# Values' projection moved to the head of a decoder layer, and its first weights loaded by a second queue

## The chip, the cores and the metric

The kernel runs on one core of one Trainium2 chip. The metric is device time in microseconds (us) of one execution. In the trace PE is TensorE, ACT is ScalarE, DVE is VectorE, POOL is GpSimd and SP is SyncE, which only starts transfers (DMAs) here.

## What is computed

One decoder layer for 256 rows of 1024 numbers, all in float32. Cut to what matters for the change:

```
def rmsnorm(x, g):
    y = x * rsqrt(mean(x * x, axis=-1, keepdims=True) + 1e-6)
    return y * g
...
hn = rmsnorm(x, norm_mix[i])
(aq, ak, av, bq, bkc, bvc, bks, bvs, bkw, bvw, bg, cq, ck, cv, mg) = split(hn @ w_in[i])
o_a = dilated_mixer(heads(aq), heads(ak), heads(av), tbl_a)
o_b = nsa_mixer(...)
o_c = moba_mixer(...)
merged = gates[0] * (o_a @ wb[:r0]) + gates[1] * (o_b @ wb[r0:r1]) + gates[2] * (o_c @ wb[r1:])
x = x + merged @ w_out[i]
x = x + conv_ffn(rmsnorm(x, norm_ffn[i]), ...)
return rmsnorm(x, norm_final)
```

The head of the kernel makes `aq` and `ak` (mixer A's queries and keys, 768 columns), `bkc` and `bvc` (256 columns), and `av` with `bvs` (512 columns: the values). Then A's attention begins.

## The kernel before

**Splitting.** Products run in fp32r. Each float32 operand is split into a high part (a copy rounded to fp32r, by ACT) and a low part (what the rounding left, by DVE), and a product is high by high, low by high and high by low: three matmuls. This holds for x and for the weights.

**Units.** Weights arrive as units of up to 1 MB (`Unit`, L205): one transfer into a `raw` tile (4 of them), the high part on ACT (`hi`, L220), the low part on DVE (`lo`, L224), into two pairs of `whi`/`wlo` tiles. So unit n+2 can be split only when PE has finished with unit n, and its transfer needs a free `raw` tile. SP issues all the transfers in program order.

**The head (L242 to L419).** It is written out by hand: inside `tc.manual_schedule` the instructions of PE, ACT, DVE and POOL stand on each engine in the order of the text. SP loads x's two halves of 128 rows (x0, x1), a small table for the position bias, then `a0` as two halves of 512 KB, `a1` as two halves, and `a2`. PE does 9 idle matmuls (`keep_warm`), then turns x by 16 transposes (`turn`, L282) into four PSUM tiles that each hold two chunks of 128 columns for all 256 rows. `hi_part` and `lo_part` (L312, L318) multiply by the norm's weights and split; the norm's 1/rms is not yet in. `a0_products` (L322) makes the first two of A's six chunks (128 columns each, with the weights as the stationary operand and 256 rows moving) in an order that follows the weights' arrival. POOL makes three of `a0`'s low parts. A chunk's result is multiplied by the row's 1/rms afterwards (`by_rows_rstd`, L290). The four chunks of `a1` and `a2` come from `chunk3_T` (L294): 24 matmuls of 256 columns each. Beside them x is normed into `h_parts` (`normed_rows`, `normed_hi`, `normed_lo`, L388 to L396), which every later projection reads.

**After the head** a list scheduler sets the order from the program's text and its own costs. Unit `kvc` gives two chunks by `chunk3_T` (L479), then `V1 = proj_V("v1", 512, "V1")` (L488) makes the values by rows: `by_rows` (L441) uses x's normed parts as the stationary operand and 512 weight columns as the moving one, 48 matmuls by `mm3` (L237). Then A's scores (L508), DVE's sum with the bias and maximum (L515), the exponentials on ACT (L586), transposes (L522), and the products with V1 (L541). The projections for mixer B (`chunk_T`, L421, one 512-column matmul for both parts of x and one of 256) lie between them and give PE work while DVE and ACT do A's softmax.

Of the kernel before, what the change touches and what calls it, by code (L numbers as in the profile page):

```python
# [16 lines left out]
P = 128  # L17
WARM = 9
NORMED = 3
S = 256  # L20
# [48 lines left out]
def _unit_list():  # L69

    rows = [(0, D)]
    out = [(f"a{i}", "w_in", rows, [(C_AQ + 256 * i, 256)]) for i in range(3)]
    out.append(("kvc", "w_in", rows, [(C_BKC, 256)]))
    out += [(f"v1{i}", "w_in", [(512 * i, 512)], [(C_AV, 384), (C_BVS, 128)]) for i in range(2)]
# [55 lines left out]
def decoder_layer(ctx: ExitStack, tc, x, small_b, table, w1, wts, norms, out):  # L130
# [12 lines left out]
    for t in range(NT):  # L143
        nc.sync.dma_start(xs[:, t, :], x[t * P:(t + 1) * P, :])
    g_mix, g_ffn = xs[:, 0, D:D + KC], xs[:, 1, D:D + KC]
# [59 lines left out]
    class Unit:  # L205


        def __init__(self, name, cuts=1):
# [42 lines left out]
    def s_tile():  # L251
# [12 lines left out]
    x_hi, x_lo = [raw_parts[:, :, i, :] for i in range(2)]  # L264
    xn = [act_pool.tile([P, D], F32, name=f"xn{t}") for t in range(NT)]
    turned = [p.tile([P, 512], F32, name=n).rearrange("p (c q) -> p c q", c=2)
              for p, n in ((ps_t, "t"), (ps_t, "t"), (ps_o, "o"), (ps_o, "o"))]
    xT = [turned[c // 2][:, c % 2, :] for c in range(KC)]
    tb = mix.tile([P, 4, S], F32, name="gl", bufs=4).rearrange("p a b -> p (a b)")[:32, :R_N]
    nc.sync.dma_start(tb, table)  # L270

    T = qkv.tile([P, 16, 256], F32, name="T")
# [30 lines left out]
    with tc.manual_schedule(engines={mybir.EngineType.Activation, mybir.EngineType.DVE, mybir.EngineType.Pool,  # L303
                                     mybir.EngineType.PE}):
        def split_hi(i, eng):
            sl = slice(i * 512, (i + 1) * 512)
            if eng == "v":
                nc.vector.tensor_copy(u_a0.parts[0][:, sl], u_a0.raw[:, sl])
            else:
                nc.scalar.activation(u_a0.parts[0][:, sl], u_a0.raw[:, sl], AF.Copy)  # L310

        def hi_part(c, eng):  # L312
            if eng == "v":
                nc.vector.tensor_scalar_mul(x_hi[:, c, :], xT[c], g_mix[:, c:c + 1])
# [19 lines left out]
        for c in (0, 1):  # L334
            hi_part(c, "v")
        for c in (2, 3):
            hi_part(c, "a")
        hi_part(4, "v")
        split_hi(0, "v")
        split_hi(1, "a")  # L340
        u_a0.lo(0, 4, nc.gpsimd)
        u_a0.lo(1, 4, nc.gpsimd)
        hi_part(5, "v")
        for c in (6, 7):
            hi_part(c, "a")
        split_hi(2, "v")
        split_hi(3, "a")
        a0_products(0, x_hi, range(6))
        ss = square_mean(xs[:, 1, 0:D], xn[1], "m1")
        for c in range(4):  # L350
            lo_part(c)
        a0_products(0, x_hi, range(6, KC))
        a0_products(1, x_hi, range(2))
        a0_products(0, x_lo, range(3))
        a0_products(1, x_hi, range(2, 4))
        u_a0.lo(2, 4, nc.gpsimd)
        rs.append(rstd_of([ss], "m1"))
        for i in range(2):
            u_a1.hi(i, 2)
        for c in range(4, KC):  # L360
            lo_part(c)
# [8 lines left out]
        u_a0.lo(3, 4)  # L370
        a0_products(0, x_lo, range(3, KC))
# [3 lines left out]
        a0_products(1, x_hi, range(4, KC))  # L375
        for i in range(2):
            u_a1.lo(i, 2)


        whole = [mix.tile([P, 4, S], F32, name="gl", bufs=4) for _ in range(2)]  # L380
        h_parts = act_pool.tile([P, KC, 2, S], F32R, name="hn")
        h_hi, h_lo = h_parts[:, :, 0, :], h_parts[:, :, 1, :]

        def weighted_rows(i):
            for c in range(4 * i, 4 * i + 4):
                nc.scalar.activation(whole[i][:, c % 4, :], xT[c], AF.Copy, scale=g_mix[:, c:c + 1])
# [11 lines left out]
        def projected(u, c):  # L398
            return chunk3_T(lambda part, k: u.views[part][:, k, c * P:(c + 1) * P], x_hi, x_lo)

        weighted_rows(0)
        nc.scalar.activation(rows_m, pt[:, :S], AF.Copy)
        u_a2.hi(0, 2)
        for c in range(2):
            by_rows_rstd(c, a0_ps[c])
        weighted_rows(1)
        u_a2.hi(1, 2)
        normed_rows(0)
        by_rows_rstd(2, projected(u_a1, 0))
        normed_rows(1)  # L410
        normed_hi(0)
        for i in range(2):
            u_a2.lo(i, 2)
# [673 lines left out]
```

## Time and profile before

| | us |
|---|---|
| median of 3 runs | 424.87 (424.62 to 425.62) |
| the profiled execution, its own time | 424.76 |
| its span in the trace | 423.0 |
| PE busy in the span | 412.4 |
| DVE busy | 313.2 |
| ACT busy | 256.2 |
| first product of a projection starts on PE | 9.22 |
| A's first scores start | 44.49 |

All times of rows count from the start of the span. The profiled execution took 1.76 us more than its span. PE's busy time counts pipelined matmuls with modelled ends, so a row's duration is longer than the step from one matmul to the next; a step is read from the starts of neighbouring rows.

### The profile page before, as it was taken

Reading aid. Unit: us, or ns where it says so; the run is one execution under the profiler, and the core shown is the slowest. Engines: PE = TensorE matmul, PEld = TensorE weight load, DVE = VectorE, ACT = ScalarE, POOL = GpSimd, SP = SyncE. Lnnn points to the kernel's source line nnn. Section 1 sums busy time; section 2 is a strip of 40 time slices with the busy share of each in tenths; the row PEclk is TensorE's granted clock in tenths of the full one; section 3 lists DMA queues with packets and bytes.
Section 4 is the critical chain, followed back from the end, with each engine's and each line's share of the span. In section 5 each row is a group of like instructions: output and inputs, shape, how many; then the busy total and the mean of one; then the engine's idle time right before and its main releaser. Section 6 shows DMA issues by size and latency. Waiting matters only on the chain.

```text
span 423.0 us, 6337 instructions
## 1 busy us (share of the span) xinstructions
PE 412.4 (98%) x2407; PEld 347.8 (82%) x2407; DVE 313.2 (74%) x624; ACT 256.2 (61%) x451; POOL 18.3 (4%) x28
## 2 busy tenths in 40 slices
PE   8999999999999999999999999999999999999993
PEld 7998778776667888878788998988888888888883
DVE  3996653788784888434753899998797797887765
ACT  5843283547787855555434889467476576584633
POOL 2500010120000000000000000000000000000001
PEclk9999999999999999999999999999999999999998
DMA  8999419532227793645350465565652743800002
GB/s 279 416 375 407 146 34 354 198 131 100 101 100 248 292 381 109 229 184 198 107 192 0 149 253 198 200 251 200 245 212 105 283 187 110 299 0 2 0 2 99
DMA packets 12750, 78.00 MB, mean 184 GB/s; under 512 B 1408, under 2 KB 1424, under 8 KB 4912
## 3 DMA queue, kind: packets, MB, share of 16 engines
q1 hardware_dynamic: 12144, 75.48, 47.8%
q0 software_dynamic: 576, 2.12, 1.4%
q8 instruction: 19, 0.31, 0.3%
q14 instruction: 11, 0.09, 0.1%
HBM read 76.52 MB, written 1.07 MB: 183 GB/s over the span
## 4 chain that ended last, share of the span: by engine, by line
PE 82%; DVE 8%; ACT 5%; DMA 2%; issue 2%; SPq 0%; POOLq 0%; POOL 0%; ACTq 0%
PE g L988 12%; PE g L239 10%; PE g L240 10%; PE g L238 10%; PE g L990 6%; PE acc L238 6%; PE acc L240 6%; PE acc L239 6%; PE g L298 3%; DVE wlo L226 2%; PE g L888 2%; PE o L541 2%; DMA raw<-in_wts_dram 2%; PE g L426 2%; PE g L300 1%
## 5 line engine op out<-in xcount | busy, mean ns | idle before, releaser
L226 DVE TENSOR_TENSOR wlo<-raw,whi 128x1024 fp32r<-128x1024 f32 (+2 forms) x131 | 154.1, 1201 | 41.0 <-ACT whi L222 40.6
L222 ACT ACTIVATE whi<-raw 128x1024 fp32r<-128x1024 f32 (+2 forms) x130 | 130.2, 1040 | 50.5 <-PE g L240 34.3
L988 PE MATMUL g<-parts,whi 128*128 128x512 f32 x256 | 89.4, 396 | 0.0
L990 PE MATMUL g<-parts,wlo 128*128 128x256 f32 x256 | 66.2, 279 | 0.0
L988 PEld LDWEIGHTS g<-parts,whi 128*128 128x128 f32 x256 | 46.7, 188 | 9.2
L990 PEld LDWEIGHTS g<-parts,wlo 128*128 128x128 f32 x256 | 48.2, 188 | 2.8
L239 PE MATMUL g<-wlo,hn 128*128 128x512 f32 (+1 forms) x128 | 50.0, 391 | 0.0
L240 PE MATMUL g<-whi,hn 128*128 128x512 f32 (+1 forms) x128 | 50.0, 391 | 0.0
L238 PE MATMUL g<-whi,hn 128*128 128x512 f32 (+1 forms) x128 | 49.8, 390 | 0.0
L967 DVE SCALAR_TENSOR_TENSOR cy<-xn,small_b,cy 128x255 f32<-128x255 f32 (+1 forms) x88 | 41.5, 480 | 9.0 <-ACT cy L965 8.0
L238 PE MATMUL acc<-whi,fl 128*128 128x512 f32 (+1 forms) x88 | 34.2, 389 | 0.1
L239 PE MATMUL acc<-wlo,fh 128*128 128x512 f32 (+1 forms) x88 | 34.0, 386 | 0.0
L240 PE MATMUL acc<-whi,fh 128*128 128x512 f32 (+1 forms) x88 | 34.0, 386 | 0.0
L965 ACT ACTIVATE cy<-xn,small_b 128x256 f32<-128x256 f32 x44 | 25.8, 598 | 7.4 <-DVE xn L997 7.4
L239 PEld LDWEIGHTS g<-wlo,hn 128*128 128x128 f32 x128 | 24.1, 188 | 5.1 <-issue 0.9
L240 PEld LDWEIGHTS g<-whi,hn 128*128 128x128 f32 x128 | 24.1, 188 | 4.2 <-issue 0.2
L238 PEld LDWEIGHTS g<-whi,hn 128*128 128x128 f32 x128 | 24.1, 189 | 4.0 <-ACT whi L222 0.2
L426 PE MATMUL g<-hn,whi 128*128 128x512 f32 x72 | 26.2, 405 | 0.0
L996 ACT ACTIVATE xn<-g 128x256 f32<-128x256 f32 x32 | 12.2, 380 | 22.2 <-PE g L988 22.2
L428 PE MATMUL g<-hn,wlo 128*128 128x256 f32 x72 | 19.9, 292 | 0.0
L997 DVE TENSOR_TENSOR xn<-g,xn 128x256 f32<-128x256 f32 x32 | 13.5, 421 | 8.3 <-ACT xn L996 8.3
L240 PEld LDWEIGHTS acc<-whi,fh 128*128 128x128 f32 x88 | 16.5, 188 | 3.4
(213 smaller groups left out, 698.6 us busy)
## 6 DMA issues: line engine op xcount, KB each, us to landing
raw<-in_wts_dram SPq DMA_DIRECT2D x61, 1024.0 KB, 4.8
gl<-in_w_dram SPq DMA_DIRECT2D x8, 512.0 KB, 7.6
raw<-in_wts_dram SPq DMA_DIRECT2D x5, 512.0 KB, 7.4
raw<-in_wts_dram SPq DMA_DIRECT2D x2, 804.0 KB, 9.0
T<-tvd POOLq DMA_DIRECT2D x1, 1280.0 KB, 16.3
xs<-in_x_dram SPq DMA_DIRECT2D x2, 516.0 KB, 3.8
out_dram<-raw SPq DMA_DIRECT2D x4, 256.0 KB, 2.1
T<-tvd POOLq DMA_DIRECT2D x1, 768.0 KB, 9.6
```

What stands on the lines that cost most here:

```text
L222: nc.scalar.activation(self.parts[0][:, sl], self.raw[:, sl], AF.Copy)
L226: return (eng or nc.vector).tensor_sub(self.parts[1][:, sl], self.raw[:, sl], self.parts[0][:, sl].bitcast(F32))
L238: nc.tensor.matmul(ps, al, bh, start=start, stop=False)
L239: nc.tensor.matmul(ps, ah, bl, start=False, stop=False)
L240: nc.tensor.matmul(ps, ah, bh, start=False, stop=stop)
L426: hi = lambda: nc.tensor.matmul(ps, view(0, k), h_parts[:, k].rearrange("p a q -> p (a q)"), start=k == 0, stop=k == KC - 1)
L428: lo = lambda: nc.tensor.matmul(ps[:, :S], view(1, k), h_hi[:, k, :], start=False, stop=False)
L965: on_act.append(nc.scalar.activation(y, u, AF.Identity, bias=vec_c[:, 3, ch:ch + 1], scale=vec_c[:, 2, ch:ch + 1]))
L967: nc.vector.scalar_tensor_tensor(y[:, sh:], u[:, :S - sh], vec_c[:, w, ch:ch + 1], y[:, sh:], op0=ALU.mult, op1=ALU.add)
L988: hi = lambda: nc.tensor.matmul(ps, u[0][:, k, cols], h_parts[:, k].rearrange("p a q -> p (a q)"), start=k == 0, stop=k == KC - 1)
L990: lo = lambda: nc.tensor.matmul(ps[:, :S], u[1][:, k, cols], h_parts[:, k, 0, :], start=False, stop=False)
L997: nc.vector.tensor_add(v, ps[:, :S], part)
```

## The change

The values' projection becomes the first one. Units `v10` and `v11` (each 512 of the 1024 rows of the weights by 512 columns) are laid out and loaded first; the first half of `v10` is issued by ACT's queue, while SP issues x0, x1, the second half of `v10`, the table, `v11`, and later `a0`, `a1`, `a2` whole. Each half of x is now turned by itself: `turned[t]` has two PSUM tiles of four chunks for 128 rows; `weighted(t, i)` (DVE) multiplies four chunks by the norm's weights into SBUF, `raw_hi_part` (ACT) and `raw_lo_part` (DVE) split them. PE multiplies x0's first two chunks with `v10` before it turns x1. The values are scaled by 1/rms on ACT as they leave PSUM. A's six chunks then all come from the normed rows `h_parts`: `chunk_products` uses 8 matmuls of 512 columns and 8 of 256 a chunk in place of 24 of 256, and `chunk_sum` adds the two halves (one instruction on ACT, one on DVE). POOL makes no low parts. `proj_V` for V1 is gone from its old place.

```diff
-WARM = 9
+WARM = 8
+PAUSE = 2
...
-    out = [(f"a{i}", "w_in", rows, [(C_AQ + 256 * i, 256)]) for i in range(3)]
+    out = [(f"v1{i}", "w_in", [(512 * i, 512)], [(C_AV, 384), (C_BVS, 128)]) for i in range(2)]
+    out += [(f"a{i}", "w_in", rows, [(C_AQ + 256 * i, 256)]) for i in range(3)]
...
-                nc.sync.dma_start(self.raw[:, sl], src[:, sl])
+                (nc.sync if i else first).dma_start(self.raw[:, sl], src[:, sl])
...
+    turned = [[p.tile([P, 512], F32, name=n).rearrange("p (c q) -> p c q", c=4) for _ in range(2)]
+              for p, n in ((ps_t, "t"), (ps_o, "o"))]
...
+    load_x(1)
+    u_v = [Unit("v10", cuts=2, first=nc.scalar)]
     nc.sync.dma_start(tb, table)
-    u_a0 = Unit("a0", cuts=2)
-    u_a1 = Unit("a1", cuts=2)
-    u_a2 = Unit("a2")
+    u_v.append(Unit("v11"))
...
+        def weighted(t, i):
+            nc.vector.tensor_mul(whole[i][:, :, t * P:(t + 1) * P], turned[t][i],
+                                 g_mix[:, 4 * i:4 * i + 4, None].to_broadcast([P, 4, P]))
...
+        def value_products(t, ks, part):
+
+            for k in ks:
+                u = u_v[k // 4]
+                for a in (raw_hi, raw_lo)[:2 - part]:
+                    nc.tensor.matmul(V1_ps[t], a[:, k, t * P:(t + 1) * P], u.views[part][:, k % 4, :],
+                                     start=part == 0 and a is raw_hi and k == 0, stop=part == 1 and k == KC - 1)
...
+        def chunk_products(u, c):
+
+            ps = psg.tile([P, 512], F32, name="g")
+            cols = slice(c * P, (c + 1) * P)
+            for k in range(KC):
+                nc.tensor.matmul(ps, u.views[0][:, k, cols], h_parts[:, k].rearrange("p a q -> p (a q)"),
+                                 start=k == 0, stop=False)
+            for k in range(KC):
+                nc.tensor.matmul(ps[:, :S], u.views[1][:, k, cols], h_hi[:, k, :], start=False, stop=k == KC - 1)
+            return ps
...
         keep_warm(WARM)
-        rs = [rstd_of([square_mean(xs[:, 0, 0:D], xn[1], "m0")], "m0")]
         turn(0)
+        weighted(0, 0)
+        raw_hi_part(0, 0)
+
+        nc.vector.tensor_copy(u_v[0].parts[0][:, 0:512], u_v[0].raw[:, 0:512])
+        u_v[0].hi(1, 4)
+        raw_lo_part(0, 0)
+        for i in range(2):
+            u_v[0].lo(i, 4)
+        s0 = square_mean(xs[:, 0, 0:D], xn[1], "m0")
+        keep_warm(PAUSE)
+        value_products(0, range(2), 0)
         turn(1)
         nc.tensor.matmul(pt[:16, :384], tb[:, R_RB:R_RB + 16], tb[:, R_OH:R_OH + 384], start=True, stop=True)
...
+        weighted(1, 0)
+        raw_hi_part(1, 0)
+        weighted(0, 1)
+        raw_lo_part(1, 0)
+        value_products(1, range(2), 0)
...
-
-    V1 = proj_V("v1", 512, "V1")
```

**Place 1: PE at the start of the program.** `g<-tt` are the idle matmuls, `<-ident,xs` the transposes, `gl 16x384` the product with the bias table. Before:

```order
L288 MATMUL g<-tt 128x128 x9
L284 MATMUL t<-ident,xs 128x128 x4
L284 MATMUL o<-ident,xs 128x128 x4
L284 MATMUL t<-ident,xs 128x128 x4
L284 MATMUL o<-ident,xs 128x128 x4
L332 MATMUL g<-gl 16x384
L325 MATMUL g<-parts,whi 128x256
L325 MATMUL s<-parts,whi 128x256
```

and with the change:

```order
L298 MATMUL g<-tt 128x128 x8
L294 MATMUL t<-ident,xs 128x128 x8
L298 MATMUL g<-tt 128x128 x2
L329 MATMUL g<-whi,parts 128x512 x4
L294 MATMUL o<-ident,xs 128x128 x8
L375 MATMUL g<-gl 16x384
L329 MATMUL s<-whi,parts 128x512 x4
L329 MATMUL g<-wlo,parts 128x512 x2
L329 MATMUL s<-wlo,parts 128x512 x2
```

The first four products now stand ahead of x1's transposes and of the table's product, which moved behind them.

**Place 2: DVE while the values are multiplied.** `parts` is x's split, `gl` the weighted rows, `hn` the normed split, `wlo` a weight's low part. Before, from the low parts of x on:

```order
L319 SCALAR_TENSOR_TENSOR parts<-t,xs,parts 128x256 x4
L177 TENSOR_SCALAR msm_221<-ssm_196 128x1
L319 SCALAR_TENSOR_TENSOR parts<-o,xs,parts 128x256 x4
L363 TENSOR_TENSOR tt<-g,gl 16x384
L226 TENSOR_TENSOR wlo<-raw,whi 128x512
L226 TENSOR_TENSOR wlo<-raw,whi 128x1024 x2
L292 SCALAR_TENSOR_TENSOR aT_130<-g,xn_105 128x256
L292 SCALAR_TENSOR_TENSOR aT_131<-s,xn_105 128x256
L389 TENSOR_TENSOR gl<-gl,xn_105 128x1024
```

and with the change, from just behind `weighted(1, 0)`, the first instruction that reads x1's transposes, to the low parts of `a0` (the last row's third is `a1`'s):

```order
L312 TENSOR_TENSOR gl<-t,xs 128x4x128
L321 TENSOR_TENSOR parts<-gl,parts 128x4x128
L312 TENSOR_TENSOR gl<-o,xs 128x4x128
L230 TENSOR_TENSOR wlo<-raw,whi 128x512 x2
L181 TENSOR_SCALAR msm_188<-ssm_154 128x1
L321 TENSOR_TENSOR parts<-gl,parts 128x4x128 x2
L181 TENSOR_SCALAR msm_198<-ssm_192 128x1
L400 TENSOR_TENSOR tt<-g,gl 16x384
L230 TENSOR_TENSOR wlo<-raw,whi 128x1024 x2
L333 TENSOR_TENSOR gl<-gl,xn_105 128x1024 x2
L340 TENSOR_TENSOR hn<-gl,hn 128x4x256 x2
L230 TENSOR_TENSOR wlo<-raw,whi 128x1024 x3
```

The norming of x (`gl<-gl,xn` and `hn<-gl,hn`) stood between results of A's chunks; now it stands ahead of `a0`'s low parts, and so ahead of A's first chunk.

**Place 3: PE where A's scores begin** (`s<-aT`; `hn,whi 128x256` are products of `kvc`). Before, the values' products end there:

```order
L238 MATMUL g<-whi,hn 128x512
L239 MATMUL g<-wlo,hn 128x512
L240 MATMUL g<-whi,hn 128x512
L508 MATMUL s<-aT_133,aT_130 128x128 x2
L508 MATMUL s<-aT_133,aT_130 128x256 x2
L426 MATMUL g<-hn,whi 128x512
L428 MATMUL g<-hn,wlo 128x256 x2
```

and with the change:

```order
L350 MATMUL g<-hn,wlo 128x256 x8
L304 MATMUL g<-hn,whi 128x256 x16
L306 MATMUL g<-hn,wlo 128x256 x8
L530 MATMUL s<-aT_361,aT_292 128x128 x2
L530 MATMUL s<-aT_361,aT_292 128x256 x2
L304 MATMUL g<-hn,whi 128x256 x16
L306 MATMUL g<-hn,wlo 128x256 x8
L530 MATMUL s<-aT_381,aT_313 128x128 x2
```

The second chunk of `kvc` moved behind the first scores. Between the last of A's three pairs of scores and the first transposes of its softmax PE has 28 chunk products with the change and 25 before. From the gates' projections on (127 us in the trace of before) every engine's order is the same.

## Rows read from the trace of the kernel before

**Rows 1.** The page: busy time by engine, and the chain that ended last.
```profile
PE 412.4 (98%) x2407; PEld 347.8 (82%) x2407; DVE 313.2 (74%) x624; ACT 256.2 (61%) x451; POOL 18.3 (4%) x28
...
PE 82%; DVE 8%; ACT 5%; DMA 2%; issue 2%; SPq 0%; POOLq 0%; POOL 0%; ACTq 0%
```

**Rows 2.** Stretches: us, length, busy PE, PEld, DVE, ACT, POOL, clock, DMA share, GB/s.
```profile
3.00:4.00 1.00, 1.00 (x7) 1.00 (x6) 0.00 (x0) 0.00 (x0) 0.00 (x0) 1.00 1.00 405
...
44.50:66.00 21.50, 21.37 (x164) 15.81 (x164) 12.90 (x42) 11.78 (x24) 2.20 (x3) 1.00 0.32 117
66.00:127.00 61.00, 59.41 (x412) 44.93 (x411) 47.50 (x196) 39.42 (x108) 5.32 (x6) 1.00 0.42 154
```

**Rows 3.** Timeline of the start: start, us, engine, line, what [idle before <-releaser].
```profile
1.00 4.21 PE L288 MATMUL g<-tt 128*128 128x128 f32 x18 [1.00 <-POOL tt L257]
...
4.07 1.06 ACT L170 ACTIVATE xn<-xs 128x1024 f32<-128x1024 f32 x1 [1.84 <-DMA xs<-in_x_dram]
...
4.79 0.87 PEld L284 LDWEIGHTS t<-ident,xs 128*128 128x128 f32 x4
...
6.46 0.47 PEld L284 LDWEIGHTS t<-ident,xs 128*128 128x128 f32 x4
...
7.54 0.81 PE L332 MATMUL g<-gl 32*16 32x384 f32 x2
...
8.73 0.63 ACT L310 ACTIVATE whi<-raw 128x512 fp32r<-128x512 f32 x1 [0.68 <-DMA raw<-in_wts_dram]
...
9.22 0.39 PE L325 MATMUL g<-parts,whi 128*128 128x256 f32 x1 [0.86 <-DVE whi L308]
...
10.01 0.63 ACT L310 ACTIVATE whi<-raw 128x512 fp32r<-128x512 f32 x1
...
10.87 0.39 PE L325 MATMUL g<-parts,whi 128*128 128x256 f32 x1 [0.43 <-DVE whi L308]
```

**Rows 4.** Timeline, PE: steps of chunks, of the values' products, and the scores.
```profile
14.81 0.60 PE L374 MATMUL g<-ident,rsm 128*128 128x128 f32 x4
...
18.13 1.12 PE L300 MATMUL g<-parts,wlo 128*128 128x256 f32 x8
...
19.09 2.08 PE L298 MATMUL g<-parts,whi 128*128 128x256 f32 x16
...
33.49 0.40 PE L238 MATMUL g<-whi,hn 128*128 128x512 f32 x1
...
44.17 0.39 PE L240 MATMUL g<-whi,hn 128*128 128x512 f32 x1
...
44.49 0.93 PE L508 MATMUL s<-aT,aT 64*128 64x128 f32 x8
...
45.34 0.50 PE L426 MATMUL g<-hn,whi 128*128 128x512 f32 x1
```

**Rows 5.** Timeline, DVE and ACT: the kinds of instruction that the change uses.
```profile
8.73 0.43 DVE L308 CAST whi<-raw 128x512 fp32r<-128x512 f32 x1 [0.47 <-DMA raw<-in_wts_dram]
...
10.01 0.80 DVE L308 CAST whi<-raw 128x512 fp32r<-128x512 f32 x1 [0.46 <-DMA raw<-in_wts_dram]
...
13.93 0.53 DVE L363 TENSOR_TENSOR tt<-g,gl 16x384 f32<-16x384 f32 x1
...
39.15 2.01 ACT L222 ACTIVATE whi<-raw 128x1024 fp32r<-128x1024 f32 x2 [4.42 <-PE g L240]
...
40.25 2.36 DVE L226 TENSOR_TENSOR wlo<-raw,whi 128x1024 fp32r<-128x1024 f32 x2 [2.50 <-ACT whi L222]
...
42.64 0.69 DVE L457 COPY V<-g 128x512 f32<-128x512 f32 x1
...
71.19 1.29 DVE L226 TENSOR_TENSOR wlo<-raw,whi 128x512 fp32r<-128x512 f32 x2 [1.72 <-ACT whi L222]
```

**Rows 6.** DMA issues in the first 50 us: count, KB, median us to landing.
```profile
T<-tvd POOLq DMA_DIRECT2D x1, 1280.0 KB, 16.3
```

**Rows 7.** Waits of PE, 44 to 130 us: us in total, times, longest.
```profile
PE t L522 <- DVE tt L566: 0.9, 3, 0.3
```

More of the change, by code (lines that the diff above doesn't have):

```diff
@@ L142, in decoder_layer, with load_x @@
     xs = act_pool.tile([P, NT, D + KC], F32, name="xs")
-    for t in range(NT):
+    def load_x(t):
         nc.sync.dma_start(xs[:, t, :], x[t * P:(t + 1) * P, :])
+    load_x(0)
     g_mix, g_ffn = xs[:, 0, D:D + KC], xs[:, 1, D:D + KC]
@@ L205, in decoder_layer, with __init__ @@
     class Unit:
-        def __init__(self, name, cuts=1):
+        def __init__(self, name, cuts=1, first=nc.sync):
             at, k, n = places[name]
@@ L328, in decoder_layer, with chunk_sum @@
+        def chunk_sum(ps):
+            j = len(aT)
+            scale = 0.125 if j < 3 else 1.0
+            part = halves[j % 2][:, :S]
+            nc.scalar.activation(part, ps[:, S:], AF.Copy, scale=scale)
+            aT.append(qkv.tile([P, S], F32, name=f"aT{j}"))
+            nc.vector.scalar_tensor_tensor(aT[j], ps[:, :S], scale, part, op0=ALU.mult, op1=ALU.add)
         keep_warm(WARM)
-        rs = [rstd_of([square_mean(xs[:, 0, 0:D], xn[1], "m0")], "m0")]
         turn(0)
+        weighted(0, 0)
@@ L336, in decoder_layer @@
[L336 to L357, printed above, removed]
+        weighted(1, 0)
[3 more added lines that the diff above has]
+        value_products(1, range(2), 0)
+        for i in (2, 3):
+            u_v[0].hi(i, 4)
+        for t in range(NT):
+            value_products(t, range(2), 1)
+        weighted(1, 1)
+        for i in (2, 3):
+            u_v[0].lo(i, 4)
@@ L358, in decoder_layer @@
+        rs = [rstd_of([s0], "m0")]
+        s1 = [square_mean(xs[:, 1, :D], xn[1], "m1")]
+        for t in range(NT):
+            raw_hi_part(t, 1)
+        for t in range(NT):
+            raw_lo_part(t, 1)
+        rs.append(rstd_of(s1, "m1"))
         for i in range(2):
-            u_a1.hi(i, 2)
-        for c in range(4, KC):
-            lo_part(c)
+            u_v[1].hi(i, 2)
+        for t in range(NT):
+            value_products(t, range(2, 4), 0)
         dm = att.tile([P, 384], F32, name="tt", bufs=3)[:16, :]
@@ L369, in decoder_layer @@
                                                       ap=[[1, P], [384, h1 - h0], [1, 256]]))
[L370 to L371 removed]
+        for i in range(2):
+            u_v[1].lo(i, 2)
+        for t in range(NT):
+            value_products(t, range(2, 4), 1)
         for t in range(NT):
             nc.tensor.matmul(pt[:, t * P:(t + 1) * P], rs[t].to_broadcast([P, P]), ident, start=True, stop=True)
[L375 to L377 removed]
@@ L380, in decoder_layer @@
[L380 to L386, printed above, removed]
-        def normed_rows(i):
-            nc.vector.tensor_mul(whole[i], whole[i], rows_m[:, None, :].to_broadcast([P, 4, S]))
@@ L404, in decoder_layer @@
[L404 to L407, printed above, removed]
+        nc.scalar.activation(rows_m, pt[:, :S], AF.Copy)
+        for t in range(NT):
+            value_products(t, range(4, KC), 0)
+        u_a = [Unit("a0")]
         normed_rows(0)
-        by_rows_rstd(2, projected(u_a1, 0))
+        u_a[0].hi(0, 2)
         normed_rows(1)
         normed_hi(0)
-        for i in range(2):
-            u_a2.lo(i, 2)
-        normed_hi(1)
-        by_rows_rstd(3, projected(u_a1, 1))
@@ L416, in decoder_layer @@
-        normed_lo(0)
-        by_rows_rstd(4, projected(u_a2, 0))
-        normed_lo(1)
-        by_rows_rstd(5, projected(u_a2, 1))
+        normed_lo(0)
+        normed_hi(1)
+        normed_lo(1)
+        u_a[0].hi(1, 2)
+        for t in range(NT):
+            value_products(t, range(4, KC), 1)
+        for i in range(2):
+            u_a[0].lo(i, 2)
+        for t in range(NT):
+            nc.scalar.activation(V1[:, t, :], V1_ps[t], AF.Copy, scale=rs[t])
+        for n in (1, 2):
+            u_a.append(Unit(f"a{n}"))
+            for i in range(2):
+                u_a[n].hi(i, 2)
+            ps = [chunk_products(u_a[n - 1], 0)]
+            u_a[n].lo(0, 2)
+            chunk_sum(ps[0])
+            u_a[n].lo(1, 2)
+            chunk_sum(chunk_products(u_a[n - 1], 1))
@@ L421, in chunk_T @@
+        for c in range(2):
+            chunk_sum(chunk_products(u_a[2], c))
     def chunk_T(view, name, scale=1.0):
```

63 lines of the change are left out of this document (23 added, 40 removed).

## The prediction

> **What bounds the kernel now.** Read the page first: PE is busy 98% of the span and makes 82% of the chain that ended last, DVE 8% [rows 1]. So time is won or lost where PE starts late, waits, or has less to do. Then the timeline of the start. The first projection product runs at 9.22 us, after 0.86 us of waiting for weights, and PE waits again until 10.87 for the second half unit [rows 3]. From there it streams through the head: its first four score matmuls start at 44.49 and the next product at 45.34 [rows 4]. I use 45.34 as the mark: until then PE has done A's six chunks, `kvc`'s two, the values, and the first scores. With the change the same work is done by the moment at which the first scores end. Behind the mark PE still waits a little (21.37 us busy of 21.5, then 59.41 of 61) [rows 2]. The sum is made against the profiled execution, 424.76 us, which is 0.11 under the median of the runs. About 0.2% (0.85 us) is what a measurement can tell from no change.
>
> **PE's work.** Steps, from row to row: eight 256-column products take 19.09 - 18.13 = 0.96, so 0.12 each; the 47 steps of 512 columns from 33.49 to 44.17 take 10.68, so 0.227 each [rows 4].
> - Before, from 9.22 to 45.34, 36.1 us: 144 x 0.12 = 17.3 (A), 48 x 0.12 = 5.8 (`kvc`), 48 x 0.227 = 10.9 (values), 0.45 for the rows' 1/rms (a row of 0.60 with its tail), 0.85 for the scores [rows 4]. That is 35.3, so 0.8 us were waits, most of them ahead of 10.87.
> - With the change A is 48 x 0.227 + 48 x 0.12 = 16.7: 0.6 less. But x1's eight transposes (0.47 for four at the high clock, so 0.95) and the table's product (0.81 with its tail, some 0.65 in steps) [rows 3] were done before 9.22 and now stand behind the first four products: 1.6 more inside the stretch. In sum 36.3 from the first product on, without any wait.
>
> **When the first product starts.** It needs x0, half a unit of weights, four transposes, and one instruction each of DVE and ACT. Before, x0 was alone in the queue and landed at 4.07. Now half a unit, as large, is in flight with it; one more half unit cost 1.28 us before (8.73 to 10.01) [rows 3]. So x0 lands between 4.07 and 5.35. I take 5.2, near the upper end, as the transfers already ran at 405 GB/s with one queue and a DMA share of 1.00 [rows 2]. The Trainium skill, "DMA: Bandwidth & Descriptors", section "Issuing engines are not separate DMA queues", says that transfers started by different engines interleave on the same 16 DMA engines and that only issue time is saved; by it x0 would land at the upper end, 5.35, and the sum below would be 425.55, where with 4.07 it would be 424.95. Four transposes at the low clock (0.87 for four) and the last one's tail end near 6.3. DVE's `weighted` reads 512 columns from PSUM (0.69, as the copy of the values) [rows 5], ACT's high part takes 0.63 [rows 3], and with some 0.1 us at each handover the first product starts at 7.85. That is 1.4 us earlier than before. The second needs the low part of x0, another 0.7; the four are through at 9.3. If x0 lands at 4.07, the eight idle matmuls (to 4.75) [rows 3] hold the transposes, and all is 0.45 earlier.
>
> **The wait that takes over.** x1's transposes stand behind those four products, so DVE's `weighted(1, 0)` starts at 9.3 + 0.75 = 10.05. From it to `a0`'s last low part DVE has no gap to speak of: 8 instructions of 512 columns (three weighted, three low parts of x, two of weights) at 1.29 / 2 = 0.645, 8 of 1024 (two low parts of `v11`, four for norming x, two of `a0`) at 2.36 / 2 = 1.18, the table's 0.53 and two small ones of 0.1 [rows 5]. That is 5.2 + 9.4 + 0.7 = 15.3, to 25.35. ACT keeps ahead, at 1.0 for 1024 columns [rows 5]. A's first chunk needs `a0`'s last low part for its last four products (0.5), so it ends at 25.9. PE alone would be there at 7.85 + 10.9 + 1.6 + 0.45 + 2.8 = 23.6: 2.3 us of waits, at the low part of x0 (0.5), at x1's high and low parts (1.1), and ahead of the first chunk's end (0.7). Then five chunks (13.9), `kvc` (5.8) and the scores (0.85) run without a gap, each unit's 5.6 us on PE being longer than its 3.4 on ACT and DVE: the mark is passed at 46.4, **1.1 us later than before**.
>
> **Edits that cost nothing, and their cover.** The table now lands behind 2.2 MB; before, that amount had landed at 10.01 [rows 3], and PE asks for it at 10.3. It could be 0.6 later unseen, since PE then waits for x1's high part. `v11` follows 1 MB later, at 12.6, and is split from 14.6 on; `a0` and `a1` have more room. The bias tile's transfers start some 2 us later (DVE's table sum at 16 in place of 13.93 [rows 5]) and land at 38 in place of 36 (16.3 us [rows 6]); the scores want them at 43.5. `chunk_sum`'s ACT copies and the values' copies (from DVE to ACT) lie under PE's chunks. POOL's low parts go, and no one waits for them.
>
> **Behind the mark.** Between A's last scores and its first transposes PE now has 28 products, 3 more than before, about 0.5 us of cover. The waits there were 0.9 us in three by the wait view, which leaves out tails [rows 7]. I take 0.5 of gain; bounds are 0 and 1.0. The order of mixer B's attention (66 to 127) also differs, with 61 - 59.41 = 1.6 us of PE idle before [rows 2] that could shrink or nearly double; I take 0 for it. From 127 on the order is the same.
>
> **Sum:** 424.76 + 1.1 - 0.5 = 425.4 us, chance 0.48. Its own range, with x0 early (-0.45) or DVE's path 0.5 longer and the cover at its bounds, is 424.4 to 426.4; 0.30 of the chance lies within 0.2%, 0.18 above.
>
> **Rivals.**
> - *Faster: DVE's path is shorter than its rows say.* If PE waited only for x0's low part (0.5), the mark would be passed at 7.85 + 36.3 + 0.5 = 44.65, 0.7 earlier, and with the 0.5 of cover the time is 423.6. For it: the cast took 0.80 while POOL's low parts ran and 0.43 without [rows 5], and POOL now rests. Against: the 0.645 and 1.18 are rows in which POOL did nothing. It needs a path of 13.6 in place of 15.3. Chance 0.28, of it 0.21 faster, 0.07 the same.
> - *Slower: the clock stays low.* Before, transposes took 0.87 for four at 4.79 and 0.47 at 6.46, so the clock rose from the lower of its two levels (1.2 GHz) to the higher (2.4) at about 6.3, though the granted clock of the row 3 to 4 us says 1.00 [rows 2, 3]; PE had been at work since 1.00 without a break, 5.3 us. Now its work ends at 4.75, pauses until x0, and pauses again ahead of the first product. Priced with that stretch again, low until 13.1, what PE does until then (eight products, transposes, table: 3.4 us) takes twice as long; x1's transposes come 1.3 later and DVE's path with them: 425.4 + 1.6 = 427.0, and 428.8 if none of it is hidden. It decides if x0's transposes and the two idle matmuls don't hold the clock. The trace of before can't tell: the clock rose during transposes, but behind 4 us of matmuls. Chance 0.11.
> - *The reordered attention decides* (61 us in which PE idled 1.6): 1.3 either way, 424.1 or 426.7. Chance 0.13: 0.04 the same, 0.06 slower, 0.03 faster.
>
> **Numbers.** Faster 0.21 + 0.03 = 0.24; the same 0.30 + 0.07 + 0.04 = 0.41; slower 0.18 + 0.11 + 0.06 = 0.35. The range reaches down into the first rival and up to the second's lower price: 423.4 to 427.0.
>
> **What the profile after would show.** Right: x0's first reader at 5.0 to 5.4, the first value product near 7.9, DVE full from 10 to 25 with PE waiting for `wlo` of `a0` ahead of the first chunk's end, the first scores' end near 46.4. Wrong: the mark ahead of 45.3, x0 near 4.1, or PE without gaps between 11 and 26 (first rival); 512-column products 0.4 us apart (second); equal marks and a different end (third).

## The result, and the profile after

The changed kernel takes **428.47 us** (median of 6 runs, 427.78 to 430.47) beside 424.78 of the kernel before: ratio 1.0092 [1.0066, 1.0118]. It is slower, by 3.7 us, and outside the range that was given. The first profile caught the slowest of the six, 430.47 us with a span of 428.7. The page's busy times and chain, which answer to [rows 1]:

```profile
PE 416.8 (97%) x2361; PEld 347.5 (81%) x2361; DVE 313.7 (73%) x620; ACT 257.4 (60%) x452; POOL 14.8 (3%) x25
...
PE 83%; DVE 8%; ACT 5%; issue 2%; DMA 1%; POOLq 0%; POOL 0%; ACTq 0%
```

PE has 46 instructions fewer and is busy 4.4 us longer. PE's timeline of the start shows where this profile lost time, beside [rows 3]:

```profile
6.63 1.06 PE L294 MATMUL t<-ident,xs 128*128 128x128 f32 x8 [2.04 <-DMA xs<-in_x_dram]
...
8.70 2.38 PE L329 MATMUL g<-whi,parts 128*128 128x512 f32 x4 [0.26 <-ACT parts L317]
10.88 1.91 PE L294 MATMUL o<-ident,xs 128*128 128x128 f32 x8
12.71 1.46 PE L375 MATMUL g<-gl 32*16 32x384 f32 x2
```

x0 is there at 6.63, after a wait of 2.04 us, where 5.2 was forecast. Its transposes run 0.12 us apart, x1's 0.23: the clock fell between them. The stretches show both, the delay and the fall (columns as in [rows 2]; the first line is from the kernel before, the others from this run):

```profile
2.00:3.00 1.00, 1.00 (x7) 1.00 (x6) 0.42 (x3) 0.22 (x2) 0.00 (x0) 1.00 0.80 305
...
2.00:3.00 1.00, 1.00 (x7) 1.00 (x6) 0.42 (x3) 0.66 (x2) 0.00 (x0) 1.00 0.64 160
3.00:4.00 1.00, 1.00 (x7) 1.00 (x6) 0.00 (x0) 0.00 (x0) 0.00 (x0) 1.00 0.96 366
...
8.00:16.00 8.00, 7.74 (x22) 4.63 (x21) 6.10 (x12) 5.50 (x11) 0.01 (x1) 0.50 1.02 400
```

Two queues moved 160 GB/s between 2 and 3 us (305 in the kernel before, whose next microsecond stands in [rows 2]), and from 8 to 16 us the granted clock was 0.50, the lower level. The other five runs have a mean clock of 0.995 to 0.997 (this one 0.983) and take 427.78 to 429.88 us, so the fall of the clock isn't what makes the median. The same kernel was therefore profiled once more.

### The profile page after: what moved, and what is told of

It is laid out like the page before. It is cut to its first block, busy times and chain, and to the rows that moved or that the text cites. A ratio compares the mean times of both kernels' runs of the same rounds, so it can differ in the third digit from the quotient of the medians.

```text
span 428.7 us, 6238 instructions
## 1 busy us (share of the span) xinstructions
PE 416.8 (97%) x2361; PEld 347.5 (81%) x2361; DVE 313.7 (73%) x620; ACT 257.4 (60%) x452; POOL 14.8 (3%) x25
## 4 chain that ended last, share of the span: by engine, by line
PE 83%; DVE 8%; ACT 5%; issue 2%; DMA 1%; POOLq 0%; POOL 0%; ACTq 0%
PE g L1010 12%; PE g L242 9%; PE g L244 9%; PE g L243 9%; PE g L1012 6%; PE acc L242 6%; PE acc L243 6%; PE acc L244 6%; PE g L450 3%; PE g L347 2%; DVE wlo L230 2%; PE g L910 2%; PE g L329 2%; PE g L452 2%; PE s L329 2%
## 5 line engine op out<-in xcount | busy, mean ns | idle before, releaser
L230 DVE TENSOR_TENSOR wlo<-raw,whi 128x1024 fp32r<-128x1024 f32 (+2 forms) x134 | 156.0, 1189 | 45.3 <-ACT whi L226 44.7
L226 ACT ACTIVATE whi<-raw 128x1024 fp32r<-128x1024 f32 (+2 forms) x133 | 131.7, 1030 | 43.3 <-PE g L244 26.5
L242 PE MATMUL g<-whi,hn 128*128 128x512 f32 (+1 forms) x112 | 43.8, 393 | 0.0
L244 PE MATMUL g<-whi,hn 128*128 128x512 f32 (+1 forms) x112 | 43.6, 390 | 0.0
L243 PE MATMUL g<-wlo,hn 128*128 128x512 f32 (+1 forms) x112 | 43.6, 389 | 0.0
L242 PEld LDWEIGHTS g<-whi,hn 128*128 128x128 f32 x112 | 21.0, 189 | 4.2 <-issue 0.8
L243 PEld LDWEIGHTS g<-wlo,hn 128*128 128x128 f32 x112 | 21.1, 188 | 4.0 <-issue 0.3
L244 PEld LDWEIGHTS g<-whi,hn 128*128 128x128 f32 x112 | 21.1, 189 | 3.6
```

What stands on the lines that cost most here:

```text
L226: nc.scalar.activation(self.parts[0][:, sl], self.raw[:, sl], AF.Copy)
L230: return (eng or nc.vector).tensor_sub(self.parts[1][:, sl], self.raw[:, sl], self.parts[0][:, sl].bitcast(F32))
L242: nc.tensor.matmul(ps, al, bh, start=start, stop=False)
L243: nc.tensor.matmul(ps, ah, bl, start=False, stop=False)
L244: nc.tensor.matmul(ps, ah, bh, start=False, stop=stop)
```

## Experiments

Three theories stood first. One: x0's lateness is the loss, and the second queue is its cause. Two: the new order of the work alone costs it. Three: the clock's fall, behind PE's pause, makes it.

### The changed kernel again

No edit.

> The changed kernel once more, beside the next one. Its first profile was of the slowest of its six runs, with a granted clock of 0.50 from 7.7 to some 18 us, and x0 there at 6.63. If x0's lateness alone makes the median, a profile with the clock at 1.00 shows x0 at 6.3 to 6.7, the first product at 8.5 to 8.8, the second scores at 47.5 to 48.5 (50.48 in the first profile, 46.19 on one queue), and 427.8 to 428.7 us. If the clock's fall is the rule in this kernel, it is there again, with the second scores past 50 and 429 us or more.

428.11 us (428.01 to 429.32), ratio 1.0090 [1.0075, 1.0105]. PE's timeline; in this profile the clock did not fall once it had risen:

```profile
6.55 1.94 PE L294 MATMUL t<-ident,xs 128*128 128x128 f32 x8 [1.77 <-DMA xs<-in_x_dram]
...
9.08 1.70 PE L329 MATMUL g<-whi,parts 128*128 128x512 f32 x4
...
23.75 1.98 PE L347 MATMUL g<-hn,whi 128*128 128x512 f32 x8
25.56 1.45 PE L350 MATMUL g<-hn,wlo 128*128 128x256 f32 x8
26.85 2.00 PE L347 MATMUL g<-hn,whi 128*128 128x512 f32 x8
...
41.23 2.08 PE L304 MATMUL g<-hn,whi 128*128 128x256 f32 x16
...
48.12 0.93 PE L530 MATMUL s<-aT,aT 64*128 64x128 f32 x8
```

x0 is as late (6.55), and the mark is 48.12. The mark is the start of the second scores here: the second chunk of `kvc` stands behind the first scores, so the work that the kernel before has done at 45.34 is done only then, and not at the first scores' end, where the prediction put it. This is the profile to set against the prediction: 2.8 us late at the mark, where the kernel before has 45.34 [rows 4]. The first product, 9.08, came later than expected, since x0's transposes ran at the low speed here: the trace's records of the granted clock begin at 9.57 us, with 1.00, and what a view prints ahead of its first record is no record.

### Every early load on SyncE's queue

SyncE issues x0, the first half unit, x1, the second half unit.

```diff
...
-    load_x(1)
-    u_v = [Unit("v10", cuts=2, first=nc.scalar)]
+    u_v = [Unit("v10", cuts=2, between=lambda: load_x(1))]
```

> The changed kernel with the same four first transfers (x0, first half of v10, x1, second half of v10) all issued by SyncE, in this order. Theory 1 (the second queue delays x0: it landed at 6.63 us, the half unit alone would have cost 1.28): x0 lands at 4.1 to 4.5, PE does not idle ahead of the transposes, the first product starts at 7.0 to 7.5 in place of 8.70, and the time falls by 1.5 to 3 against the change, to 425.5 to 427. Theory 2 (the order of the work alone costs it: x1's transposes behind the products and x's norming ahead of a0's low parts): x0 lands early but the time stays over 427.5. Theory 3 (the clock's fall alone): the time falls only if the 512-column steps of the values' products are 0.23 from the first on.

426.16 us (425.68 to 426.55), ratio 1.0006 [0.9983, 1.0029]. PE's timeline:

```profile
4.57 1.92 PE L295 MATMUL t<-ident,xs 128*128 128x128 f32 x8
...
7.39 1.48 PE L330 MATMUL g<-whi,parts 128*128 128x512 f32 x4 [0.19 <-DVE whi L367]
8.72 1.03 PE L295 MATMUL o<-ident,xs 128*128 128x128 f32 x8
...
10.67 0.81 PE L376 MATMUL g<-gl 32*16 32x384 f32 x2 [0.92 <-DMA gl<-in_table_dram]
...
46.19 0.93 PE L531 MATMUL s<-aT,aT 64*128 64x128 f32 x8
```

x0's transposes start behind the warming passes, without a wait for it. The mark is 1.93 us earlier than in the changed kernel and the time about 2.1 us shorter. So the loads make the larger part of the loss; the order of the work is the same in both kernels. This edit both takes the second queue away and sets the half unit ahead of x1; the late half, further down, parts the two.

### More idle matmuls in the changed kernel

```diff
-WARM = 8
-PAUSE = 2
+WARM = 14
+PAUSE = 5
```

> The changed kernel with 14 idle matmuls ahead of x0's transposes in place of 8 and 5 behind them in place of 2, so that PE works until x0 is there and until the first product. Theory 3 (the clock fell because PE idled from 4.6 to 6.6): the granted clock stays 1.00 from 7.5 to 18, steps are 0.23, and the time falls by 2 to 3.5 against the change, to 425 to 426.5. Theory 1 (late x0): x0 still lands at 6.6, first product still near 8.5, the time falls by no more than 1, to 427.5 or above. Theory 2 (order): as theory 1, with DVE busy without gaps from x1's transposes to a0's low parts.

427.97 us (427.66 to 429.09), ratio 1.0058 [1.0037, 1.0079].

```profile
6.54 1.06 PE L294 MATMUL t<-ident,xs 128*128 128x128 f32 x8
...
8.61 0.50 PE L329 MATMUL g<-whi,parts 128*128 128x512 f32 x1
```

PE is kept busy up to x0, the clock stays high, the transposes run 0.12 apart, and the time is within 0.5 us of the changed kernel's. The pause of PE is not what the median loses by.

### The kernel before, with a second queue

```diff
...
-    u_a0 = Unit("a0", cuts=2)
+    u_a0 = Unit("a0", cuts=2, first=nc.scalar)
```

> The kernel before with one part of the change alone: the first half of a0 is issued by ScalarE's queue. Theory 1 (two queues slow each other down more than their bytes say): x0 lands near 6.6 in place of 4.07 and the first 2 us of transfers run below 300 GB/s in place of 355; PE idles ahead of its transposes; the first product, which needs all of x and the half unit, starts 0 to 1 later than 9.22 and the time is 0 to 1 more, 424.8 to 425.8. If transfers of two queues only share the rate, x0 lands at 5.2 to 5.4 and the time is within 0.5. Theory 3: if PE's pause brings the clock down as in the changed kernel, products take twice as long and the time is 2 or more longer, 427 and above.

427.75 us, ratio 1.0047 [1.0027, 1.0067]. ACT's and PE's timeline:

```profile
6.26 1.06 ACT L170 ACTIVATE xn<-xs 128x1024 f32<-128x1024 f32 x1 [3.58 <-DMA xs<-in_x_dram]
6.37 1.09 PE L284 MATMUL t<-ident,xs 128*128 128x128 f32 x4 [1.16 <-DMA xs<-in_x_dram]
...
11.12 0.39 PE L325 MATMUL g<-parts,whi 128*128 128x256 f32 x1
```

x0 lands 2.2 us later than in [rows 3] (4.07), with no change of order, and the first product is 1.9 us late. Three of the ten runs have a mean clock of 0.995 or 0.996 and take 425.67 to 426.49 us, seven have 0.987 to 0.991 and take 427.6 to 428.4. So the lateness alone costs this kernel about 1 us (three runs). In the other seven the lower clock goes with 1.5 to 2 us more; the profile is of one of the three, so where the clock fell in the seven is not shown.

### The kernel before, with a pause of PE

`WARM = 4` in place of 9.

> The kernel before with 4 idle matmuls in place of 9, so PE pauses from about 2.9 to 4.8 us and nothing else changes. Theory 3 (a pause of some 2 us of PE ahead of the transposes leaves the clock low for many us): 256-column steps of 0.22 in place of 0.12 over some us, and 2 to 4 us more, 427 to 429. Theories 1 and 2: the clock does not decide, transposes are slow until 6.3 as before, and the time stays within 0.5 of 424.8.

425.73 us (424.49 to 426.55), ratio 1.0006 [0.9989, 1.0022]; the first product is at 9.02 (9.22 before). PE waits 1.20 us for x0:

```profile
4.27 1.09 PE L284 MATMUL t<-ident,xs 128*128 128x128 f32 x4 [1.20 <-DMA xs<-in_x_dram]
```

A pause of that length costs nothing that the medians tell. The profile is of the fastest run; four of the ten have a mean clock of 0.991 or 0.992 and take 425.93 to 426.55, where four of 29 of the kernel before have one below 0.994. So the pause may bring such runs more often; ten runs do not show it.

### What the second queue may carry

Five kernels change only the loads; all have the changed order. The first two start from the kernel with one queue, the others from the changed kernel.

x0 by two queues, cut at column `HC = 512`:

```diff
...
+            nc.scalar.dma_start(xs[:, 0, 0:HC], x[0:P, 0:HC])
+            nc.sync.dma_start(xs[:, 0, HC:], x[0:P, HC:])
```

> As the changed kernel with every early load on SyncE's queue (426.16 us, its x0 there by 4.57), but x0 alone is cut in two by columns: 512 of them by ScalarE's queue, 520 by SyncE's, and all else stays behind on SyncE's. No byte more stands ahead of x0. Theory 1 (what is in flight at the same time shares the engines, so that x0 is late by the bytes of the half unit beside it): here only x0's own halves share, x0 is there by 4.3 to 4.8, and the time is 425.7 to 426.6. Theory 2 (a second queue in use from the first microsecond slows the start itself, whatever it carries): some 170 GB/s between 2 and 3 us again, x0 at 5.5 or later, 427.3 to 428.5 us.

The table alone by ScalarE's queue:

```diff
-    nc.sync.dma_start(tb, table)
+    nc.scalar.dma_start(tb, table)
```

> As the changed kernel with every early load on SyncE's queue, but the small table (98 KB, 32 partitions) goes by ScalarE's queue. Theory 1 (shared by bytes): 98 KB at some 300 GB/s put x0 0.3 us later, under the warming passes that run until 4.5, so its transposes start by 4.9; the table is there before its product, whose wait of 0.92 us at 10.67 goes; 425.3 to 426.2 us. Theory 2 (the second queue slows the start, whatever it carries): x0 at 5.5 or later, 427 to 428 us.

The half unit issued by ScalarE behind its first activation (`late` holds the transfer):

```diff
-    nc.scalar.activation(warm, half, AF.Exp)
...
+        nc.scalar.activation(warm, half, AF.Exp)
+        u_v[0].late()
         keep_warm(WARM)
```

> As the changed kernel, but ScalarE issues the half unit behind its table load and first activation, at some 2.3 to 2.7 us in place of 0.74; SyncE's queue goes on with x0, x1 and the rest. Theory 1: x0 has moved for the most part when the half unit's packets begin, and is there by 4.6 to 5.0; the half unit shares with x1 and the second half and is there at 7.0 to 7.8, so the first product starts at 7.3 to 8.1 (8.70 in the changed kernel, 7.39 on one queue) and the time is 425.8 to 427.2 us. Theory 2, if it holds for a queue's first use at any time: a drop in the rate of moved bytes about 4 us, x0 at 5.3 or later, 427.2 to 428.5 us.

A quarter, 256 KB, by ScalarE's queue (`first`), the next quarter by SyncE's ahead of x1:

```diff
...
+                    first.dma_start(self.raw[:, :mid], src[:, :mid])
+                    nc.sync.dma_start(self.raw[:, mid:sl.stop], src[:, mid:sl.stop])
+                    load_x(1)
...
-    load_x(1)
```

> As the changed kernel, but ScalarE's queue carries half of what it did ahead of x1: 256 KB of weights in place of 512; the other 256 KB follow x0 on SyncE's queue, ahead of x1. If x0 is late by the bytes beside it, it stands between the 98 KB run (5.17 us) and the changed kernel (6.63), near 5.6 (5.3 to 5.9), and the time near 427.0 us (426.4 to 427.6). If any larger transfer beside x0 makes the whole delay, x0 is there at 6.2 to 6.7 and the time is 427.6 to 428.6 us.

The two queues exchanged, with the half unit by SyncE's:

```diff
-        nc.sync.dma_start(xs[:, t, :], x[t * P:(t + 1) * P, :])
+        (nc.sync if t else nc.scalar).dma_start(xs[:, t, :], x[t * P:(t + 1) * P, :])
...
```

> The two first transfers change queues: x0 by ScalarE's queue, the half unit of weights by SyncE's, x1 and the rest behind it; the same bytes start at the same moment. ScalarE's table load again stands behind its issue (1.17 us). If the two transfers hinder each other whichever queue they are in, or if the table load behind the issue does it, x0 is there at 5.8 to 6.8 us and the time is 427.3 to 428.6 us. If the loser is SyncE's queue alone, because ScalarE's is served first, x0 is there by 4.8, the half unit is late (first product at 8 or later), and the time is 426.0 to 427.5 us.

x0's transposes are read from PE's timelines (one profile a kernel, two of the changed one), "held" where no wait for x0 is listed and the warming passes ended last; GB/s is that of 2 to 3 us:

| kernel | ScalarE's queue | issued | x0's transposes | GB/s | time, us |
|---|---|---|---|---|---|
| one queue | nothing | - | 4.57, held | 281 | 426.16 |
| x0 by two queues | 256 KB of x0 | 0.74 | 4.52, held | 320 | 426.01 |
| late half | 512 KB of weights | 0.91 | 4.75, held | 355 | 426.27 |
| table second | 98 KB | 0.74 | 5.17 | 130 | 426.43 |
| quarter | 256 KB of weights | 0.74 | 6.83 | 138 | 427.64 |
| changed kernel | 512 KB of weights | 0.74 | 6.63, 6.55 | 160, 181 | 428.47, 428.11 |
| swapped | 516 KB, x0 itself | 0.74 | 6.65 | 156 | 428.85 |

Three of the rows, of x0 by two queues, the late half and the quarter:

```profile
4.52 1.06 PE L300 MATMUL t<-ident,xs 128*128 128x128 f32 x8
...
4.75 1.92 PE L296 MATMUL t<-ident,xs 128*128 128x128 f32 x8
...
6.83 1.06 PE L299 MATMUL t<-ident,xs 128*128 128x128 f32 x8 [2.11 <-DMA xs<-in_x_dram]
```

The delay does not go by bytes: 256 KB make x0 as late as 512. It isn't the second queue as such either, since x0's own halves on two queues are there in time. Nor is SyncE's queue the loser: on ScalarE's, x0 is as late.

The DMA view counts packets, the pieces in which a transfer moves. The quarter's two queues from 3 to 5 us (`q1` is SyncE's, `q10` ScalarE's; packets, MB, share of the engines' time):

```profile
q1 hardware_dynamic: 82, 0.33, 46.7%
q10 hardware_dynamic: 82, 0.17, 43.1%
```

The queues' packets went one for one, though ScalarE's were half as long; in the changed kernel the counts are 78 and 83. At these lengths (2 and 4 KB) the quarter's 256 KB are as many packets as the half unit's 512 KB, 128. That would be why both cost x0 the same: by packets, not by bytes. The table, with some 3 KB a packet only a quarter as many, costs less (5.17). It is read from few profiles, and it doesn't explain the low rate between 2 and 3 us.

The late half is the surprise. It was meant to be issued at 2.3 us or later; ScalarE's queue does not wait for the table load to end, and the issue moved by 0.17 us only:

```profile
0.74 1.28 ACT L363 ACT_TABLE_LOAD   x1 [0.74 <-PEq L1099]
0.91 0.38 ACTq L223 DMA_DIRECT2D raw<-in_wts_dram  x1
```

In the changed kernel the order is the other one:

```profile
0.74 0.40 ACTq L221 DMA_DIRECT2D raw<-in_wts_dram  x1
...
1.17 1.28 ACT L154 ACT_TABLE_LOAD   x1 [1.17 <-PEq L1095]
```

The same 512 KB in the same queue then cost x0 nothing, and 2.2 us of time were back (ratio to before 1.0028 [1.0018, 1.0039], where the changed kernel has 1.0092). Its packets tell more. Between 2 and 3 us only SyncE's move (86); from 3.6 to 5, with x1 waiting behind x0 in SyncE's queue, it is ScalarE's turn:

```profile
q10 hardware_dynamic: 70, 0.29, 90.6%
q1 hardware_dynamic: 6, 0.00, 0.2%
```

So here the three transfers moved one behind the other in the order of their issue (x0, half unit, x1), across both queues, and x0 shared with little; issued in the same moment, the two first ones alternate. The table load stands behind the issue, at 1.17, in x0 by two queues as well, and x0 is in time there, at 320 GB/s: that place alone does not slow a start. Why the rate between 2 and 3 us is low only where x0 shares with another tensor's transfer stays open.

### The same issue order in the kernel before

The edit is that of the late half, on `u_a0`.

> The kernel before with the first half of a0 by ScalarE's queue (427.75 us, x0 there at 6.3), but issued behind ScalarE's first table load, as in the run of the changed kernel in which that moved the issue by only 0.17 us, to 0.91, and took the whole delay away. If the cause is the start of two queues at the same moment or the table load behind the issue, x0 is there by 4.8 and the time is 424.5 to 425.6 us. If that run owed its gain to something else and the bytes beside x0 count, x0 is there at 5.5 or later and the time is 426.5 to 428 us.

427.93 us (426.67 to 428.23), ratio 1.0058 [1.0032, 1.0083]. ACT's and PE's timeline:

```profile
4.91 1.06 ACT L169 ACTIVATE xn<-xs 128x1024 f32<-128x1024 f32 x1 [2.68 <-DMA xs<-in_x_dram]
...
8.48 0.91 PE L286 MATMUL t<-ident,xs 128*128 128x128 f32 x4 [2.25 <-DMA xs<-in_x_dram]
```

x0 is there at 4.91, as that order would have it, 1.35 us earlier than with the issue at 0.74. But x1 now comes behind the half unit (from 4 to 5 us 52 packets of ScalarE's queue moved and 7 of SyncE's), and this kernel's first product needs both row blocks: x1's transposes wait 2.25 us, and the clock falls behind that wait (0.50 from 10 to 14 us). The expected time was wrong, the expected x0 right. The changed order can use x0 alone; the old one can't. The kernel's five runs have mean clocks of 0.987 to 0.994, so the fall is likely in most of them.

### The order alone: a later table

On one queue, with the first row block's low products and the second's first products ahead of the table's product:

```diff
         turn(1)
-        nc.tensor.matmul(pt[:16, :384], tb[:, R_RB:R_RB + 16], tb[:, R_OH:R_OH + 384], start=True, stop=True)
+        value_products(0, range(2), 1)
...
-        for t in range(NT):
-            value_products(t, range(2), 1)
+        nc.tensor.matmul(pt[:16, :384], tb[:, R_RB:R_RB + 16], tb[:, R_OH:R_OH + 384], start=True, stop=True)
+        value_products(1, range(2), 1)
```

> As the changed kernel with every early load on SyncE's queue, but TensorE takes the table's product behind the second row block's first products and does the first row block's two products with low weights ahead of them. If TensorE is the bound from 7.4 us to the second scores, its one wait of 0.92 us goes whole: second scores at 45.2 to 45.6 in place of 46.19, and 424.9 to 425.5 us. If VectorE's path (the low parts of the normed rows, at its end by 22.04) bounds as closely, less than 0.3 us goes: second scores at 45.9 to 46.2, 425.8 to 426.3 us.

426.18 us (425.86 to 428.09), ratio 1.0033 [1.0021, 1.0046]: nothing won. PE's timeline:

```profile
10.64 0.49 PE L330 MATMUL s<-whi,parts 128*128 128x512 f32 x1 [0.54 <-ACT parts L318]
11.37 0.96 PE L330 MATMUL s<-whi,parts 128*128 128x512 f32 x3 [0.23 <-DVE parts L322]
12.26 0.81 PE L384 MATMUL g<-gl 32*16 32x384 f32 x2
13.00 0.87 PE L330 MATMUL s<-wlo,parts 128*128 128x512 f32 x2
13.67 1.91 PE L330 MATMUL g<-whi,parts 128*128 128x512 f32 x4
```

The wait for the table (0.92) became waits for x1's high and low part (0.54 and 0.23), made by ACT and DVE. This profiled run (427.80, mean clock 0.993) is one of two of twelve with a low mean clock; in it the clock fell at 13.43 us, so its mark can't be used. At 13.67 it has done the work that one queue has done at 13.39, and the fall, 0.24 us earlier, can have cost 0.12 of the 0.28: nothing is won up to there. That VectorE's path takes over is the likely reading, not shown at the mark.

## Why the prediction was wrong

- **x0 "between 4.07 and 5.35": this step failed.** The upper end was the time of one more half unit within one queue, 1.28 us [rows 3], and the reasoning was by bytes. Measured: 6.55 and 6.63, since the two transfers, issued in the same moment, moved packet by packet in turn and at a lower rate (160 and 181 GB/s between 2 and 3 us, 305 before). The Trainium skill, "DMA: Bandwidth & Descriptors", section "Issuing engines are not separate DMA queues", says that transfers of several engines interleave on the same engines and only issue time is saved. The changed kernel's trace agrees on the interleaving (78 and 83 packets); the late half's does not, where the transfers moved one behind the other. The estimate of 5.35 that the prediction made from that rule fell short by 1.2. Where x0 is in time, the time is 426.0 to 426.4 us, inside the range that was given: the second queue costs some 2 us, and it is what put the result outside.
- **The path behind x0 was sized well.** x0 was 1.35 us late against 5.2, the first product 1.23 (9.08 for 7.85) and DVE's first `weighted` of x1 1.20 (11.25 for 10.05). From there to `a0`'s last low part DVE took 14.9 us, forecast 15.3 (14.9 on one queue too):

```profile
11.25 0.69 DVE L312 TENSOR_TENSOR gl<-o,xs 128x512 f32<-128x512 f32 x1 [0.29 <-PE o L294]
...
23.86 3.49 DVE L230 TENSOR_TENSOR wlo<-raw,whi 128x1024 fp32r<-128x1024 f32 x3
```

  (two of the three rows' instructions are `a0`'s, to 26.19). The second chunk starts at 26.85, 0.95 later than forecast, as the path took back 0.4.
- **"Without a gap" was 0.7 short.** From the second chunk to the mark it is 21.3 us (48.12 - 26.85, and 21.2 on one queue) where 20.55 was summed: five chunks take 14.4 for 13.9, `kvc` and the scores 6.9 for 6.65. Of the 0.7, 0.3 is one wait ahead of the fifth of these chunks: DVE, held up by `a2`'s low parts, had not yet read the chunk whose PSUM tile the next one needs.

```profile
PEld g L347 <- DVE aT L359: 0.3, 1, 0.3
```

  The rest is spread over the rows' ends. On one queue the two errors cancel: 0.95 early at the second chunk, 46.19 for 46.4 at the mark. That this mark agrees is partly luck.
- **"0.5 of gain" behind the mark failed in sign, and by a misread row.** The three waits of [rows 7] are not between A's last scores and its first transposes, where the three products were to cover them. They stand at 96, 109 and 117 us, in mixer B's softmax (its tile is `tt`); A's own transposes (tile `t`) waited for nothing. Before:

```profile
56.25 0.43 PE L522 MATMUL t<-ident,t 128*128 128x128 f32 x2
...
96.39 0.30 PE L522 MATMUL t<-ident,tt 128*128 128x128 f32 x1 [0.31 <-DVE tt L566]
```

  So there was nothing to cover. From the mark to the end of the span it is 378.2 us (426.3 - 48.12) where before it was 377.7 (423.0 - 45.34): 0.5 lost. It is no chance of one profile: the ten profiles with the changed order have 378.1 to 378.3, the four with the old one 377.6 to 377.7. The stretches with equal work (the same 577 matmuls in all) tell where, before and in the second profile:

```profile
45.34:65.68 20.34, 20.21 (x156) 15.02 (x154) 12.21 (x41) 11.03 (x24) 2.20 (x3) 1.00 0.29 105
65.68:128.75 63.07, 61.48 (x425) 46.24 (x424) 47.50 (x196) 39.91 (x109) 5.32 (x6) 1.00 0.41 151
...
48.12:68.46 20.34, 20.13 (x155) 15.01 (x154) 12.46 (x37) 10.70 (x24) 2.20 (x3) 1.00 0.28 104
68.46:132.13 63.67, 61.92 (x426) 46.46 (x425) 47.64 (x197) 40.51 (x110) 5.24 (x6) 1.00 0.42 149
```

  A's attention, up to 65.68 and 68.46, takes 20.34 in both: the cover is worth 0.0. Mixer B's, in its new order, takes 0.6 more, where the prediction took 0. Behind it, where PE's order is the same again (from 128.75 before, a little later than the 127 of the text ahead), 0.1 comes back. Of the 0.6, 0.16 is idle time (1.59 and 1.75); DVE's three waits are there, 1.1 us in place of 0.9:

```profile
PE t L544 <- DVE tt L588: 1.1, 3, 0.5
```

  The other 0.44 lies within rows that count as busy and stays open.
- **The sum** of the second profile: 424.76 + 2.8 + 0.5 = 428.06, and its run took 428.05; the two differences come from the same spans, so this adds up by itself. Against the forecast's 1.1 and -0.5 that is 1.7 at the mark and 1.0 behind it: 1.35 for x0, less the 0.4 that DVE's path took back, 0.7 within the chunks, 1.0 behind them. x0 is the largest term, and it alone carried the time out of the range: the kernel with the table on ScalarE's queue, x0 at 5.17, took 426.43.
- **The rivals.** The faster one needed a path of 13.6 us on DVE; it took 14.9, with x0 late and in time, and on one queue the mark still came 0.85 after the old one. The clock's fall is real but rare here: one of the changed kernel's ten runs, at 430.47, some 2 us above the others (2.4 at the mark, 50.48 for 48.12, between its two prices of 1.6 and 3.4). The reordered attention went the slower way (0.6 of its 1.3), too little to decide. No rival had a transfer that comes later than its bytes say, which is what decided.
- **The order itself** is no gain: with x0 in time the four kernels beside one another measure 1.0026 to 1.0033 (ends of their intervals 1.0016 and 1.0046), some 1.1 to 1.4 us slower than before; the forecast was 0.6 with x0 at 5.2 and 0.2 with x0 early. One queue's own interval [0.9983, 1.0029] is too wide to tell. In its profile it is 0.85 at the mark and some 0.65 behind it. No version here beats the kernel before.

## What to carry to other kernels

Put the transfer that the whole start waits for where nothing else starts in the same moment, and read its landing from the trace before anything behind it is costed: two transfers that merely share bandwidth on paper cost 2 us here, and an issue 0.17 us later took that back. Bound an overlap of queues by more than the sum of bytes, since no row of a single queue shows what two do, and count packets too. Before a gain is put down for "more cover" ahead of a wait, look up in the timeline where that wait stands and which tile it is for: the waits counted here stood 40 to 60 us later, in another mixer.

## What was not expected of the hardware

- The start of two queues together, with different tensors: 130 to 181 GB/s between 2 and 3 us in the table's last four kernels, 281 to 355 in its first three, and x0 up to 2.3 us later, by no rule of bytes. The queues' packets went one for one, of 2 KB as of 4 KB (82 and 82 in the quarter).
- Transfers on two queues moved one behind the other when one was issued 0.17 us later: the half unit's packets (70 from 3.6 to 5 us) came behind x0's and ahead of x1's (6).
- ScalarE's queue issues a transfer 0.17 us after its table load begins, without waiting for the 1.28 us that the load takes.
- The clock at the start differs from run to run of one kernel: x0's eight transposes took 1.06 us in the first profile and 1.94 in the second, at the same 6.6 us, while the views print a granted clock of 1.00 in both. The traces' own records settle it: the first at 1.00 begins at 4.27 us in the first profile and at 9.57 in the second, and ahead of it 1.00 is printed without a record. In the first the clock had risen, PE then waited 2.04 us for x0, and at 7.68 the clock fell to 0.50 until 17.92; in the second it rose only behind the wait and stayed up. The Trainium skill, "TensorE: Matmul & The Clock Gate", section "What's actually happening", says that how many matmuls run at the low clock at a start varies between runs of one kernel; these two profiles agree. In the quarter's profile (430.62 us, mean clock 0.983) the same pattern stood: a rise at 4.53, a wait of 2.11, fast transposes at 6.83, then 0.50 from 7.95.
